# A decoder layer in fp32 on one core: two column parts of the output projection as one pass of Strassen's seven products

## The chip, the core and the metric

The kernel runs on one core of a Trainium2 chip. A core has a matrix engine (PE), a vector engine (DVE), an activation engine (ACT), a general engine (POOL, GpSimd) and an engine that issues most transfers (SP). Each of them works through its own list of instructions in order, and semaphores tie the lists together. All operands sit in SBUF, 128 partitions wide; PE accumulates into PSUM banks of 512 fp32 numbers per partition, which the other engines read. The metric is the device time of one execution in microseconds; lower is better.

## The reference

One layer of a hybrid decoder on 512 tokens of width 2048, all in fp32:

```python
h = rmsnorm(x, ln_mix)
sb_q, sb_k, sb_v, sw_q, sw_k, sw_v = split(h @ w_in)
sb_o = stick_breaking_attention(sb_q, sb_k, sb_v)       # 16 heads of 64
sw_o = sliding_window_sink_attention(sw_q, sw_k, sw_v, sinks, slopes)  # 16 heads, 4 kv heads
mixed = concat(rmsnorm(sb_o, sb_out_norm), rmsnorm(sw_o, swa_out_norm))
x = x + mixed @ w_out                                   # (512 x 2048) @ (2048 x 2048)
gate, up = split(rmsnorm(x, ln_ffn) @ w_gate_up)        # each 512 x 5632
x = x + (silu(gate) * up) @ w_down
return rmsnorm(x, ln_final)
```

The change is in `mixed @ w_out`, in the half that takes `rmsnorm(sw_o)`: 512 x 1024 times 1024 x 2048.

## The kernel before, in words

A matrix product in full precision is made of three matmuls. An operand is split into a rounded part hi (made by ACT as a copy) and a rest lo = operand - hi (made by DVE), and PE adds hi by hi, hi by lo and lo by hi. For weights the two parts are called whi and wlo (`split`, L221 and L222), for the mixed heads mhi and mlo, for the normed input of the feed-forward part hca, hcs, hco and hct.

Plain projections run as a queue of slabs. A slab is 256 rows by 512 columns of a weight, one transfer of 512 KB on SP's queue; its raw tile has three buffers, its whi and wlo two. With 4 token blocks, 2 row blocks and 3 matmuls a slab of the output projection has 24 matmuls of 512 columns in eight steps; four slabs make a column part (`add_outA`, `add_outB`), 96 matmuls. A split is issued one slab ahead. At the end of a part DVE evicts its four PSUM banks with x = rstd * bank + x. Between the steps, `defer(n, fn)` runs a function n steps later.

The gate, up, down and value projections don't run in this way, but as passes of Strassen's seven products with Winograd's sums: left and right operands are cut into 2 x 2 blocks, sums and differences of blocks take the place of one product in eight. In such a pass POOL makes differences of raw weights, ACT copies them to PSUM in rounded form (hp) and again to SBUF (whi), DVE makes wlo from hp. The work is laid out in slots, one for each half of a product, and functions are put at a slot with `at_slot`. The forms are the left operands: of the blocks 11, 12, 21, 22 the products 1, 2, 4 use blocks, the products 7, 5, 6, 3 use s3 = 11 - 21, s1 = 21 + 22, s2 = s1 - 11 and 12 - s2, in place.

The output projection's first half (rows of `w_out` for head group A, four column parts) is filler for the sliding-window attention: 16 blocks (4 groups by 4 token blocks), each with scores, exponentials, transposes (`swa_tr`: PE transposes s into the banks z, ACT copies them as phi, DVE makes plo), and the product with v. `pull(cost)` steps the queue of slabs until that much PE time has passed. After the last block of a group the tile oB holds the group's two head blocks; `sumsq_add` squares them on ACT (oc) and adds them on POOL to sqB, and `mix_split` makes mhi by an ACT copy with the gain as scale (L273) and mlo by a DVE operation (L274).

Then come the four column parts of the second half, `add_outB`, plain. The norm's factor rstdB is computed from sqB (8 small matmuls, L735, and a short chain on DVE and ACT) in the first of them. When a part of x is complete, `h2_split` transposes it (16 PE transposes, L1209, four DVE operations that apply gain and factor, L1214) to the tile xh. From two such tiles `form` makes the seven left operands of the feed-forward part: for s = 0 from parts 0 and 1 inside the third part, for s = 1 from parts 2 and 3 later. Sums are on DVE (L1240 and L1243) except that of product 3 (POOL, L1246), hi parts on ACT (L1253), lo parts on DVE (L1256).

The order within an engine is the compiler's schedule for instructions that are not pinned, and program order for the pinned ones (`pV`, `pA`, `pG`, `pT`, all transfers on SP). In the passes most are pinned.

## Time and profile before

| | us |
|---|---|
| runs | 1989.48, 1989.37, 1988.89 (median 1989.37) |
| profiled execution | 1988.84 |
| its span in the trace | 1987.0 |
| end of the first half's last part, and last window block | 576 to 599.8 |
| second half, parts 0 and 1 | 599.8 to 647 |
| second half, part 2, with the forms for s = 0 | 647 to 671.7 |
| second half, part 3 | from 671.7 |

The page gives per engine its busy time, its share of the span and its count of instructions; then a digit for each fortieth of the span; then the chain of work that ended last, by engine. Rows of groups read: line, engine, operation, output <- inputs, shape, xcount, then busy time and mean ns of one, then idle time ahead of them and what ended it. Timeline rows read: start in us, duration, then the same. Instructions that directly follow each other and are alike stand in one row (x4), with the duration of the whole. Matmul durations overlap: matmuls of 512 columns start every 0.227 us and are shown as 0.39 each.

### The profile page before, as it was taken

The page shows a single profiled execution, that of the slowest core. Times are in us where ns is not written, and L with a number is a line of the kernel's source. Part 1 is how long each engine was busy: PE and PEld are TensorE (multiplying, and loading weights), DVE is VectorE, ACT ScalarE, POOL GpSimd, SP SyncE. Part 2 cuts the span into 40 slices and gives each one's busy share as a digit, 9 for nine tenths or more (in the row PEclk, how much of TensorE's full clock was granted, in tenths as well). Part 3 has the DMA queues.
Part 4 walks back from the last instruction along what each step waited for, and adds up shares of the span by engine and source line. Part 5 has one row for each costly group of instructions (what it writes and reads, how often), then busy time and mean ns, then how long its engine had stood idle before and what let it go on. Part 6 is the DMA issues. An engine that isn't in the chain of part 4 may idle for free.

```text
span 1987.0 us, 28973 instructions
## 1 busy us (share of the span) xinstructions
PE 1974.1 (99%) x10204; PEld 1687.7 (85%) x10204; DVE 1480.3 (75%) x2053; ACT 1498.5 (75%) x2015; POOL 999.8 (50%) x441
## 2 busy tenths in 40 slices
PE   9999999999999999999999999999999999999998
PEld 8888888898888888888888888888888888888886
DVE  6676888889964787777777777777777867767767
ACT  6775878868753587777777777777777788888887
POOL 2840000000010266657576666657575778878883
PEclk9999999999999999999999999999999999999999
DMA  6415454422342554444545354444534734433523
GB/s 203 148 54 142 97 144 113 121 75 85 96 138 96 172 136 113 127 125 114 137 103 144 101 139 110 129 121 118 135 104 129 279 127 148 149 127 120 177 75 117
DMA packets 290977, 252.81 MB, mean 127 GB/s; under 512 B 12560, under 2 KB 234832, under 8 KB 288400
## 3 DMA queue, kind: packets, MB, share of 16 engines
q1 hardware_dynamic: 289072, 244.11, 42.2%
q0 software_dynamic: 1376, 5.52, 0.9%
q8 instruction: 81, 1.33, 0.3%
q10 hardware_dynamic: 384, 1.34, 0.2%
q14 instruction: 64, 0.52, 0.1%
HBM read 218.40 MB, written 19.92 MB: 120 GB/s over the span
## 4 chain that ended last, share of the span: by engine, by line
PE 97%; ACT 2%; DVE 1%; issue 0%; DVEq 0%; POOL 0%; ACTq 0%; POOLq 0%
PE o L118 36%; PE m L118 30%; PE m L418 3%; PE m L419 3%; PE m L420 3%; PE m L384 2%; PE m L382 2%; PE m L383 2%; PE z L118 1%; PE o L384 1%; PE o L382 1%; PE o L383 1%; PE z L933 1%; PE o L961 1%; PE z L1132 1%; PE z L886 1%
## 5 line engine op out<-in xcount | busy, mean ns | idle before, releaser
L118 DVE TENSOR_TENSOR wlo<-t,hp 128x1024 fp32r<-128x1024 f32 x247 | 301.2, 1219 | 184.6 <-PE o L118 114.2
L118 POOL TENSOR_TENSOR t<-raw,t 128x1024 f32<-128x1024 f32 x111 | 282.2, 2543 | 281.5 <-ACT hp L118 269.6
L118 ACT ACTIVATE whi<-t 128x1024 fp32r<-128x1024 f32 x247 | 262.1, 1061 | 126.4 <-PE o L118 76.4
L118 PE MATMUL o<-hca,whi 128*128 128x512 f32 x880 | 307.5, 391 | 0.0
L118 POOL TENSOR_TENSOR t<-raw,raw 128x1024 f32<-128x1024 f32 x114 | 295.0, 2590 | 21.9 <-issue 11.3
L118 DVE TENSOR_TENSOR wlo<-raw,hp 128x1024 fp32r<-128x1024 f32 x187 | 228.3, 1221 | 93.2 <-issue 52.2
L118 ACT ACTIVATE whi<-raw 128x1024 fp32r<-128x1024 f32 (+1 forms) x189 | 200.0, 1058 | 105.0 <-PE m L118 75.0
L118 ACT ACTIVATE hp<-t 128x1024 fp32r<-128x1024 f32 x247 | 249.2, 1009 | 2.9 <-POOL t L118 2.9
L118 PE MATMUL o<-hca,wlo 128*128 128x256 f32 x880 | 244.0, 280 | 0.0
L118 ACT ACTIVATE hp<-raw 128x1024 fp32r<-128x1024 f32 x191 | 192.9, 1010 | 3.8 <-DVE wlo L118 1.4
L118 PEld LDWEIGHTS o<-hca,whi 128*128 128x128 f32 x880 | 164.2, 187 | 35.8
L118 PE MATMUL m<-hca,whi 128*128 128x512 f32 x528 | 186.3, 392 | 1.1 <-DVE hca L118 1.1
L118 PEld LDWEIGHTS o<-hca,wlo 128*128 128x128 f32 x880 | 165.6, 189 | 0.4
L221 ACT ACTIVATE whi<-raw 128x1024 fp32r<-128x1024 f32 x87 | 91.9, 1057 | 86.1 <-PE o L384 38.6
L222 DVE TENSOR_TENSOR wlo<-raw,whi 128x1024 fp32r<-128x1024 f32 x87 | 109.4, 1258 | 54.7 <-ACT whi L221 52.6
L730 POOL TENSOR_TENSOR sqA<-sqA,oc 128x512 f32<-128x512 f32 x7 | 10.1, 1439 | 273.9 <-ACT oc L729 273.9
L118 PE MATMUL m<-whi,dca 128*128 128x512 f32 x592 | 146.9, 389 | 0.0
L118 PE MATMUL o<-whi,dca 128*128 128x512 f32 x592 | 146.8, 389 | 0.0
L118 PE MATMUL m<-hca,wlo 128*128 128x256 f32 x528 | 146.3, 280 | 0.0
L118 PEld LDWEIGHTS o<-whi,dca 128*128 128x128 f32 x592 | 111.1, 188 | 23.0
L118 PEld LDWEIGHTS m<-whi,dca 128*128 128x128 f32 x592 | 111.0, 188 | 23.1
L118 PE MATMUL m<-hcs,whi 128*128 128x512 f32 x352 | 125.9, 392 | 0.0
(364 smaller groups left out, 5187.5 us busy)
## 6 DMA issues: line engine op xcount, KB each, us to landing
raw<-in_w_gate_up_dram SPq DMA_DIRECT2D x348, 256.0 KB, 5.2
raw<-in_w_down_dram SPq DMA_DIRECT2D x68, 512.0 KB, 5.0
raw<-in_w_in_dram SPq DMA_DIRECT2D x35, 512.0 KB, 4.5
raw<-in_w_in_dram SPq DMA_DIRECT2D x66, 256.0 KB, 3.9
raw<-in_w_out_dram SPq DMA_DIRECT2D x32, 512.0 KB, 3.7
aT<-w SPq DMA_DIRECT2D x44, 256.0 KB, 3.4
xd<-aT SPq DMA_DIRECT2D x10, 1024.0 KB, 6.7
rx<-in_w_down_dram SPq DMA_DIRECT2D x20, 512.0 KB, 5.7
```

Of the source, the lines that this page charges most:

```text
L118: return lambda *a, **k: tc.keep_in_program_order(fn(*a, **k))
L221: A.activation(out=hi, in_=raw, func=AF.Copy)
L222: V.tensor_tensor(out=lo, in0=raw, in1=f(hi), op=ALU.subtract)
L382: mm(o, lhsT=lh[:, sl], rhs=hi[:, j, :], start=first, stop=False, skip_group_check=halves)
L383: mm(o, lhsT=lh[:, sl], rhs=lo[:, j, :], start=False, stop=False, skip_group_check=halves)
L384: mm(o, lhsT=ll[:, sl], rhs=hi[:, j, :], start=False, stop=(k == nslab * a - 1), skip_group_check=halves)
L418: mm(o, lhsT=wh, rhs=xh, start=(k == 0), stop=False)
L419: mm(o, lhsT=wh, rhs=xl, start=False, stop=False)
L420: mm(o, lhsT=wl, rhs=xh, start=False, stop=(k == KT - 1))
L886: mm(out, lhsT=kb, rhs=H.q2[:, c0:S], start=False, stop=True, skip_group_check=True)
L933: mm(zb[:, o:o + r.shape[1]], lhsT=lhsT, rhs=r, start=False, stop=last, skip_group_check=True)
L961: mm(H.ob[:, c0:S], lhsT=vb, rhs=r[:, o:o + S - c0], start=(k == 3 and r is B.h), stop=(k == 0 and r is B.l), skip_group_check=True)
```

## The change

The first two column parts of the second half become one pass of seven products (`OutPass`, a `Block` as in the other passes). Its left blocks are halves of the tokens by halves of the 1024 rows, its right blocks are the two column parts by the same halves: 7 products, 2 halves each, 12 matmuls of 512 columns per half. Four of its left operands need sums of oB, so oB must be multiplied by the gain ahead: POOL does that in place after the last block of a group. `split_b` then makes mhi and mlo of two head blocks at a time, where `mix_split` made one. The last three slabs of the first half's last part are held back from the window blocks and run in the pass's six preparatory slots, four steps in each. The parts 2 and 3 stay plain. The transposes of parts 0 and 1, their sums of squares and the forms for s = 0 move into part 2, and of these forms POOL now makes the sums of 5 and 6 and the lo parts of 1, 2, 4 and 3 in addition to the sum of 3.

```diff
+    obs = ExitStack()
+    obp = obs.enter_context(tc.tile_pool(name="obp", bufs=1))
+    oB = [obp.tile([P, 4, 512], F32, name=f"oB{n}") for n in range(2)]
     sqB = swp.tile([P, 512], F32, name="sqB", bufs=1)
-    oB = [swp.tile([P, 4, 512], F32, tag="oB", name="oB", bufs=2) for _ in range(2)]
...
+    def split_b(m):
+        hi, lo = mixB[8 + m] = (act8("mhi"), act8("mlo"))
+        for e in (0, 2):
+            A.activation(out=hi[:, e:e + 2, :], in_=oB[m][:, e:e + 2, :], func=AF.Copy)
+            V.tensor_tensor(out=lo[:, e:e + 2, :], in0=oB[m][:, e:e + 2, :], in1=f(hi)[:, e:e + 2, :], op=ALU.subtract)
+        for j in range(4):
+            mixB[4 * m + j] = (hi[:, j, :], lo[:, j, :])
...
-                sumsq_add(sqB, oB[g // 2][:, (g % 2) * 2 + j, :], g == 0 and j == 0, tmp(name="oc"))
+                o = oB[g // 2][:, (g % 2) * 2 + j, :]
+                sumsq_add(sqB, o, g == 0 and j == 0, tmp(name="oc"))
+                G.tensor_scalar(out=o, in0=o, scalar1=gcol[:, 40 + 2 * g + j:41 + 2 * g + j], scalar2=None, op0=ALU.mult)
...
-    pull(2600.0)
+    pull(2600.0, a_end - 3)
...
+        if j == 13:
+            split_b(0)
+        pull(SWFILL / 4, a_end - 3)
+    split_b(1)
+    drain(a_end - 3)
     kqs.close()
-    rstdB = sumsq_rstd(sqB, "rstdB")
...
+    class OutPass(Block):
...
+        def sum(self, p, i):
+            self.difference(p, i, self.raw["12", i] if p == "5" else self.t["6", i] if p == "4" else
+                            self.tile("t", [P, 2, 512], bufs=3))
...
+        def add(self, p, eng):
+            b = self.block
+            if p == "7":
+                self.s3 = self.tile("t", [P, 2, 512], bufs=3).rearrange("p u (a b) -> p (u a) b", a=2)
+                eng.tensor_tensor(out=self.s3, in0=b("11"), in1=b("21"), op=ALU.subtract)
+            elif p == "5":
+                eng.tensor_tensor(out=b("21"), in0=b("21"), in1=b("22"), op=ALU.add)
+            elif p == "6":
+                eng.tensor_tensor(out=b("11"), in0=b("21"), in1=b("11"), op=ALU.subtract)
+            else:
+                eng.tensor_tensor(out=b("12"), in0=b("12"), in1=b("11"), op=ALU.subtract)
+
+        def form(self, p, eng=None):
+            src = self.s3 if p == "7" else self.block({"5": "21", "6": "11", "3": "12"}[p])
+            if eng is None:
+                self.f[p] = self.tile("vf", [P, 4, 512], F32R, 2)
+                pA.activation(out=self.f[p][:, :, 0:256], in_=src, func=AF.Copy)
+            else:
+                hl = self.f[p]
+                eng.tensor_tensor(out=hl[:, :, 256:512], in0=src, in1=f(hl)[:, :, 0:256], op=ALU.subtract)
+
+        def take(self, p):
+            bk = self.bank[{"6": "1", "4": "7", "3": "5"}.get(p, p)]
+            if p == "6":
+                self.u.append(self.tile("vu", [P, 2, 512]))
+            for t in range(2):
+                if p == "6":
+                    pV.tensor_copy(out=self.u[0][:, t, :], in_=bk[t])
+                else:
+                    c, h = {"1": (0, 0), "7": (1, 2), "4": (0, 2), "5": (1, 2), "2": (0, 0), "3": (1, 0)}[p]
+                    out = x2[c][:, h + t, :]
+                    pV.scalar_tensor_tensor(out=out, in0=bk[t], scalar=rstd_b[0][:, h + t:h + t + 1], in1=out,
+                                            op0=ALU.mult, op1=ALU.add)
+
...
+    open_phase("op", 1, reuse_waits="tile")
+    bp = OutPass()
...
+    for k, q, i in ((-6, "22", 0), (-6, "12", 0), (-5, "11", 0), (-4, "11", 1), (-3, "12", 1), (-2, "22", 1),
+                    (0, "21", 0), (1, "21", 1)):
+        at_slot(k, "load", bp.load, q, i)
+    for k, fn, *args in ((-5, bp.add, "7", pG), (-4, bp.sum, "7", 0), (-3, bp.add, "5", pV), (-3, bp.sum, "5", 0),
+                         (-2, bp.form, "7", pV), (-2, bp.add, "6", pV), (-1, bp.sum, "6", 0), (-1, bp.add, "3", pV),
+                         (0, bp.sum, "7", 1), (1, bp.sum, "5", 1), (2, bp.form, "6", pG), (3, bp.sum, "6", 1),
+                         (4, bp.sum, "4", 0), (5, bp.sum, "4", 1), (6, bp.form, "5", pG), (8, bp.form, "3", pG)):
+        at_slot(k, "sum", fn, *args)
+    for k, p in ((-4, "7"), (0, "6"), (4, "5"), (7, "3")):
+        at_slot(k, "late", bp.form, p)
+    for k, p in enumerate(PD):
+        at_slot(2 * k + 2, "take", bp.take, p)
+    for k, c, h in ((8, 1, 0), (9, 0, 2), (11, 1, 2)):
+        for t in range(2):
+            at_slot(k + t, "late", bp.add_u, c, h, t)
...
+    def b_slot(n):
+        run(n, "load")
+        run(n, "sum")
+        bof(n + 1, "to_hi")
+        bof(n + 1, "to_lo")
+        bof(n + 2, "to_hp")
+
+    for n in range(-6, 0):
+        if n == -4:
+            rstd_b.append(sumsq_rstd(sqB, "rstdB", pz()))
+        if n == -2:
+            open_z("psb")
+        b_slot(n)
+        for _ in range(4):
+            step()
+        run(n, "late")
...
             elif p == "5":
                 src = a21
-                eV.tensor_tensor(out=src, in0=a21, in1=a22, op=ALU.add)
+                (eV if s else G).tensor_tensor(out=src, in0=a21, in1=a22, op=ALU.add)
             elif p == "6":
                 src = a11
-                eV.tensor_tensor(out=src, in0=a21, in1=a11, op=ALU.subtract)
+                (eV if s else G).tensor_tensor(out=src, in0=a21, in1=a11, op=ALU.subtract)
             elif p == "3":
                 src = a12
                 (pG if s else G).tensor_tensor(out=src, in0=a12, in1=a11, op=ALU.subtract)
...
-            eV.tensor_tensor(out=hl[:, :, 256:512], in0=src, in1=f(hl)[:, :, 0:256], op=ALU.subtract)
+            (G if s == 0 and p in "1243" else eV).tensor_tensor(out=hl[:, :, 256:512], in0=src, in1=f(hl)[:, :, 0:256],
+                                                                op=ALU.subtract)
...
-                if c == 1:
-                    defer(12, lambda: [form(p, 0) for p in PR])
...
-                lambda k: mixB[k], lambda: four(1), done, mix_prep(mixB, oB, 40))
-    add_outB(0)
-    outB0 = len(queue)
-    for c in range(1, 4):
+                lambda k: mixB[k], lambda: four(1), done)
+    for c in (2, 3):
         add_outB(c)
-    drain(outB0)
+    for n in range(14):
+        b_slot(n)
+        if n == 9:
+            load(a_end)
+        if n == 12:
+            load(a_end + 1)
+        if n == 13:
+            split(a_end)
+        bof(n, "product")
+        run(n, "take")
+        run(n, "late")
+    run(14, "take")
+    dma(out=x2s[0], in_=x2[0])
     phase[0].close()
+    obs.close()
     right = ExitStack()
     side = right.enter_context(tc.tile_pool(name="side", bufs=1, side="right", reuse_waits="tile"))
+    open_z("pszb")
+    defer(2, lambda: h2_split(0))
+    defer(3, lambda: [norm_sums(0, t) for t in range(NT)])
+    defer(5, lambda: dma(out=x2s[1], in_=x2[1]))
+    defer(8, lambda: h2_split(1))
+    defer(9, lambda: [norm_sums(1, t) for t in range(NT)])
+    defer(14, lambda: [form(p, 0) for p in PR])
```

Three places show how the order of the engines' lists changes. In all rows the names behind <- are inputs, and "waits" lists the engines or queues whose semaphores the instruction waits for.

The first is DVE at the end of the first half's last part. x_5944 or x_5976 is that part's x, m and o are its banks, sst to rstdB is the norm's factor. Before, from the wlo of that part's last slab:

```order
L222 TENSOR_TENSOR wlo<-raw,whi 128x1024 [waits DMAHW0_49,Activation_49]
L222 TENSOR_TENSOR wlo<-raw,whi 128x1024 [waits DMAHW1_49,Activation_49]
L1061 SCALAR_TENSOR_TENSOR x_5944<-m,rstdA,x_5944 128x512 [waits DMASW5_49,PE_49]
L1061 SCALAR_TENSOR_TENSOR x_5944<-m,rstdA,x_5944 128x512 [waits PE_49]
L1061 SCALAR_TENSOR_TENSOR x_5944<-o,rstdA,x_5944 128x512 [waits PE_49] x2
L738 COPY sst<-o 128x4 [waits PE_49]
L278 TENSOR_SCALAR rv<-sst 128x4 [waits DVE_49]
L222 TENSOR_TENSOR wlo<-raw,whi 128x1024 [waits DMAHW2_49,Activation_49]
L284 TENSOR_TENSOR rt<-rr 128x4 [waits Activation_49]
```

After, from the middle of the norm's chain; the second row ahead of oB's is the wlo of the last slab, oB_4120 and oB_4121 are the tiles of groups 0, 1 and 2, 3, the last row is the wlo of the pass's first product:

```order
L284 TENSOR_TENSOR rt<-rr 128x4 [waits Activation_49]
L285 TENSOR_TENSOR rt<-rt,rv 128x4 [waits DVE_49]
L286 TENSOR_SCALAR rt<-rt 128x4 [waits DVE_49]
L288 TENSOR_TENSOR rstdB<-rr,rt 128x4 [waits DVE_49]
L222 TENSOR_TENSOR wlo<-raw,whi 128x1024 [waits DMAHW2_49,Activation_49]
L118 TENSOR_TENSOR oB_4120<-oB_4120,oB_4121 128x4x256 [waits Pool_49]
L118 TENSOR_TENSOR vf<-t,vf 128x4x256 [waits Activation_49]
L118 TENSOR_TENSOR oB_4120<-oB_4120 128x4x256 [waits DVE_49]
L1073 SCALAR_TENSOR_TENSOR x_5976<-m,rstdA,x_5976 128x512 [waits DMASW5_49,PE_49]
L1073 SCALAR_TENSOR_TENSOR x_5976<-m,rstdA,x_5976 128x512 [waits PE_49]
L118 TENSOR_TENSOR oB_4121<-oB_4121,oB_4120 128x4x256 [waits DVE_49]
L118 TENSOR_TENSOR wlo<-rx,hp 128x1024 [waits DMAHW3_49,Activation_49]
```

The norm's chain has moved ahead of the last slab's wlo, and three sums of oB and a lo form (vf) now stand around the part's evictions.

The second place is ACT after the last block of group 2 in the window attention, before:

```order
L1122 ACTIVATE s<-s,den 128x256 [waits Activation_49]
L273 ACTIVATE mhi<-oB,gcol 128x512
L1135 ACTIVATE phi<-z 128x512 [waits PE_49]
L273 ACTIVATE mhi<-oB,gcol 128x512
L1135 ACTIVATE phi<-z 128x512 [waits PE_49]
L221 ACTIVATE whi<-raw 128x1024 [waits DMAHW3_49,PE_49]
```

and after:

```order
L1135 ACTIVATE s<-s,den 128x256 [waits Activation_49]
L1148 ACTIVATE phi<-z 128x512 [waits PE_49]
L1059 ACTIVATE mhi<-oB_4121 128x1024 [waits Pool_49]
L1148 ACTIVATE phi<-z 128x512 [waits PE_49]
L221 ACTIVATE whi<-raw 128x1024 [waits DMAHW3_49,PE_49]
```

The two scaled copies that waited for nothing new have become one of double width, which waits for POOL, with a phi behind it.

The third place is ACT in the third column part of the second half, where the rows of L221 are whi of its slabs and of the next part's first. Before:

```order
L1253 ACTIVATE hcs<-xh 128x4x256 [waits DVE_49]
L221 ACTIVATE whi<-raw 128x1024 [waits DMAHW5_49,PE_49]
L1253 ACTIVATE hca<-xh 128x4x256 [waits DVE_49]
L1253 ACTIVATE hca<-xh 128x4x256
L221 ACTIVATE whi<-raw 128x1024 [waits DMAHW6_49,PE_49,Activation_49]
L1253 ACTIVATE hca<-xh 128x4x256 [waits DVE_49]
L1253 ACTIVATE hca<-xh 128x4x256 [waits Pool_49]
L221 ACTIVATE whi<-raw 128x1024 [waits DMAHW7_49,PE_49,Activation_49]
```

After, with the forms' hi parts in other places among the whi (the last two rows are the part's fourth slab and the first slab of the next part):

```order
L1390 ACTIVATE hcs<-xh 128x4x256 [waits DVE_49,Pool_49]
L1390 ACTIVATE hcs<-s_6563 128x4x256 [waits DVE_49]
L221 ACTIVATE whi<-raw 128x1024 [waits DMAHW3_49,PE_49]
L1390 ACTIVATE hcs<-xh 128x4x256 [waits DVE_49]
L1390 ACTIVATE hca<-xh 128x4x256 [waits Pool_49]
L1390 ACTIVATE hca<-xh 128x4x256
L1390 ACTIVATE hca<-xh 128x4x256 [waits Pool_49] x2
L221 ACTIVATE whi<-raw 128x1024 [waits DMAHW6_49,PE_49]
L221 ACTIVATE whi<-raw 128x1024 [waits DMAHW7_49,DVE_49,PE_49]
```

POOL's list there, which before held one sum (L1246), is now:

```order
L1393 TENSOR_TENSOR hcs<-xh,hcs 128x4x256 [waits Activation_49]
L1377 TENSOR_TENSOR xh<-xh 128x4x256 [waits DVE_49]
L1380 TENSOR_TENSOR xh<-xh 128x4x256 [waits Pool_49]
L1393 TENSOR_TENSOR hcs<-xh,hcs 128x4x256 [waits Activation_49]
L1383 TENSOR_TENSOR xh<-xh 128x4x256 [waits Pool_49]
L1393 TENSOR_TENSOR hca<-xh,hca 128x4x256 [waits Activation_49] x2
```

The rows of L1377, L1380 and L1383 are the sums of 5, 6 and 3, those of L1393 lo parts. All seven hi parts now stand ahead of the whi of the fourth slab, the last two of them behind a wait for POOL.

More of the change, by code (lines that the diff above doesn't have):

```diff
@@ L730, in sumsq_add, with sumsq_rstd @@
             G.tensor_tensor(out=acc, in0=acc, in1=t, op=ALU.add)
-    def sumsq_rstd(acc, name):
-        pb = po()
+    def sumsq_rstd(acc, name, pb=None):
+        pb = po() if pb is None else pb
         for t in range(NT):
@@ L1067, in tile_hymba @@
         add_outA(c)
+    a_end = len(queue)
     def swa_scores(g, blk):
@@ L1176, in tile_hymba, with __init__, tile, acc @@
         at(swa_av, j - 2)
-        pull(SWFILL / 4)
+        pull(SWFILL / 4, a_end - 3)
         at(swa_norm, j)
         at(swa_scores, j + 1)
-        pull(SWFILL / 4)
-    drain()
-    kqs.close()
-    rstdB = sumsq_rstd(sqB, "rstdB")
+        if j == 13:
+            split_b(0)
+        pull(SWFILL / 4, a_end - 3)
+    split_b(1)
+    drain(a_end - 3)
+    kqs.close()
+    class OutPass(Block):
+        def __init__(self):
+            Block.__init__(self, 0, 0, 0, [], "6")
+            self.f = {}
+        def tile(self, tag, shape, dt=F32, bufs=1):
+            return phase[1].tile(shape, dt, tag=tag, name=tag, bufs=bufs)
+        def acc(self, c):
+            return x2[c]
+        def load(self, q, i):
+            r, c = int(q[0]) - 1, int(q[1]) - 1
+            if q in ("11", "21"):
+                if i == 0:
+                    self.raw[q] = o8.tile([P, 4, 512], F32, tag="o8", name="rx")
+                raw = self.raw[q][:, 2 * i:2 * i + 2, :]
+            elif q == "22":
+                raw = wp.tile([P, 2, 512], F32, tag="raw", name="raw", bufs=RAWB)
+            else:
+                raw = self.tile("raw2", [P, 2, 512], bufs=2)
+            r0 = SBW + (r * 4 + 2 * i) * P
+            dma(out=raw, in_=wout[r0:r0 + 2 * P, c * 512:(c + 1) * 512].rearrange("(a p) c -> p a c", p=P))
+            self.raw[q, i] = raw
+        def sum(self, p, i):
+            self.difference(p, i, self.raw["12", i] if p == "5" else self.t["6", i] if p == "4" else
+                            self.tile("t", [P, 2, 512], bufs=3))
+        def left(self, p, k, half, c):
+            if p in "124":
+                q = {"1": (0, 0), "2": (0, 1), "4": (1, 1)}[p]
+                c += q[0] * 256
+                return mixB[8 + q[1]][half][:, k, c:c + P]
+            c += half * 256
+            return self.f[p][:, k, c:c + P]
+        def block(self, q):
+            return oB[int(q[1]) - 1][:, :, 0:256] if q[0] == "1" else oB[int(q[1]) - 1][:, :, 256:512]
+        def add(self, p, eng):
[24 more added lines that the diff above has]
+                    pV.tensor_copy(out=self.u[0][:, t, :], in_=bk[t])
+                else:
+                    c, h = {"1": (0, 0), "7": (1, 2), "4": (0, 2), "5": (1, 2), "2": (0, 0), "3": (1, 0)}[p]
+                    out = x2[c][:, h + t, :]
+                    pV.scalar_tensor_tensor(out=out, in0=bk[t], scalar=rstd_b[0][:, h + t:h + t + 1], in1=out,
+                                            op0=ALU.mult, op1=ALU.add)
+        def add_u(self, c, h, t):
+            out = x2[c][:, h + t, :]
+            pV.scalar_tensor_tensor(out=out, in0=self.u[0][:, t, :], scalar=rstd_b[0][:, h + t:h + t + 1], in1=out,
+                                    op0=ALU.mult, op1=ALU.add)
@@ new lines, in tile_hymba, with bof @@
+    rstd_b = []
+    open_phase("op", 1, reuse_waits="tile")
+    bp = OutPass()
+    def bof(n, what):
+        if 0 <= n < 14:
+            getattr(bp, what)((PD[n // 2], n % 2))
+    for k, q, i in ((-6, "22", 0), (-6, "12", 0), (-5, "11", 0), (-4, "11", 1), (-3, "12", 1), (-2, "22", 1),
[6 more added lines that the diff above has]
+        at_slot(k, "sum", fn, *args)
```

11 lines of the change are left out of this document (7 added, 4 removed).

## The prediction

> **What bounds the kernel now.** I read the page's busy shares and chain first, then PE's own waits, then four stretches around the change: the end of the first half's fourth column part, the second half's first two parts, its third, and the start of the fourth.
>
> ```profile
> span 1987.0 us, 28973 instructions
> PE 1974.1 (99%) x10204; PEld 1687.7 (85%) x10204; DVE 1480.3 (75%) x2053; ACT 1498.5 (75%) x2015; POOL 999.8 (50%) x441
> PE 97%; ACT 2%; DVE 1%; issue 0%; DVEq 0%; POOL 0%; ACTq 0%; POOLq 0%
> ...
> PE o L118 <- POOL ones L127: 1.2, 1, 1.2
> PE m L118 <- DVE hca L118: 1.1, 1, 1.1
> ...
> 576.00:599.80 23.80, 23.80 (x111) 19.82 (x110) 11.83 (x14) 8.07 (x10) 4.19 (x4) 1.00 0.56 177
> 599.80:647.00 47.20, 47.20 (x218) 39.26 (x217) 22.95 (x29) 16.25 (x29) 0.00 (x0) 1.00 0.28 92
> 647.00:671.70 24.70, 24.70 (x119) 20.66 (x118) 20.94 (x20) 11.79 (x17) 2.40 (x1) 1.00 0.44 149
> ```
>
> PE sets the end. Its two longest waits in 1987 us are 1.2 and 1.1 us, and in these stretches it is busy all the time at clock 1.00 (columns of the last rows: us, then PE, PE loads, DVE, ACT, POOL, clock, DMA share, GB/s). So a removed matmul is worth its full pitch, and anything that makes PE wait costs its full length. POOL has nothing to do in the second stretch; the change fills it.
>
> **A, the matmuls removed.** Two column parts were 2 x 96 matmuls of 512 columns; the pass has 7 x 2 x 12 = 168.
>
> ```profile
> 624.92 1.75 PE z L1209 x16
> 648.49 1.75 PE z L1209 x16
> ```
>
> Between these two groups of transposes lies one part: (648.49 - 624.92 - 1.75)/96 = 0.227 us each. 24 fewer: **-5.45 us**. Everything else is what PE may now wait for.
>
> **How DVE and POOL stand to each other.** This decides most of the sum.
>
> ```profile
> 657.41 1.22 DVE L1243 TENSOR_TENSOR xh<-xh 128x1024 f32<-128x1024 f32 x1
> 658.94 3.33 DVE L222 TENSOR_TENSOR wlo<-raw,whi 128x1024 fp32r<-128x1024 f32 x1 [0.31 <-ACT whi L221]
> 658.78 2.40 POOL L1246 TENSOR_TENSOR xh<-xh 128x1024 f32<-128x1024 f32 x1 [72.97 <-DVE xh L1243]
> ...
> 708.16 2.38 DVE L118 TENSOR_TENSOR hca<-xh,hca 128x1024 fp32r<-128x1024 f32 x1
> 707.07 2.40 POOL L118 TENSOR_TENSOR xh<-xh 128x1024 f32<-128x1024 f32 x1 [2.25 <-DVE xh L118]
> 709.42 6.75 POOL L118 TENSOR_TENSOR t<-raw,raw 128x1024 f32<-128x1024 f32 x2
> ...
> L118 DVE TENSOR_TENSOR wlo<-t,hp 128x1024 fp32r<-128x1024 f32 x247 | 301.2, 1219 | 184.6 <-PE o L118 114.2 <-PE m L118 70.4
> L118 DVE TENSOR_TENSOR dca<-xd,dca 128x1024 fp32r<-128x1024 f32 x10 | 23.7, 2372 | 0.0
> ```
>
> A DVE operation of 1024 elements takes 1.22. When it reads both inputs from SBUF and starts under a POOL operation of 2.40, it ends 1.09 (658.94 + 3.33 - 658.78 - 2.40) or 1.07 after POOL's end: it has done all its work after POOL. POOL's two differences at 709.42 take 6.75, not 4.8: POOL waits its turn as well. So the two alternate, at about 3.5 us a pair. With one input in PSUM (hp) the mean over 247 is the plain 1.219, with two in SBUF beside a busy POOL 2.372. The Trainium skill, "SBUF — State Buffer", section "Who interferes with whom", says the same: a DVE instruction with two SBUF inputs contends with a GpSimd instruction that reads SBUF. By it the three tiny operations of the rstd chain that have two inputs would each wait for a POOL operation too; in C below the last slab's wlo would then come 6.2 late and that of product 1 only 1.8 more, 8.0 instead of 7.5.
>
> **B, the gain multiplies in the window blocks.** After the last block of a group ACT multiplied oB by gain itself; now its 1024-wide mhi waits for POOL to add a square, multiply, add, multiply, and phi, oc and the exponentials stand behind it in ACT's order.
>
> ```profile
> 551.67 2.65 POOL L730 TENSOR_TENSOR sqB<-sqB,oc 128x512 f32<-128x512 f32 x2 [27.67 <-ACT oc L729]
> 554.25 0.59 ACT L1135 ACTIVATE phi<-z 128x512 fp32r<-128x512 f32 x1
> 559.18 0.91 ACT L1122 ACTIVATE s<-s,den 128x256 f32<-128x256 f32 x2 [0.71 <-DVE den L1117]
> 560.67 1.03 PE L1132 MATMUL z<-ident,s 128*128 128x128 f32 x8
> 515.45 2.67 POOL L730 TENSOR_TENSOR sqB<-sqB,oc 128x512 f32<-128x512 f32 x2 [27.45 <-ACT oc L729]
> 520.46 0.59 ACT L1135 ACTIVATE phi<-z 128x512 fp32r<-128x512 f32 x1
> 521.08 0.69 DVE L1136 TENSOR_TENSOR plo<-z,phi 128x512 fp32r<-128x512 f32 x1
> 521.81 0.28 PE L1081 MATMUL z<-kst,qst 128*128 128x256 f32 x1
> L118 POOL TENSOR_TENSOR x2r<-x2r,gf 128x512 f32<-128x512 f32 x8 | 10.4, 1299 | 18.6 <-ACT junk L118 18.4
> L832 POOL TENSOR_SCALAR_AFFINE_SELECT dist<-dist 128x256 f32<-128x256 f32 x1 | 0.4, 410 | 0.1
> L137 POOL TENSOR_SCALAR_AFFINE_SELECT scr<-ones 128x128 f32<-128x128 f32 x1 | 0.3, 304 | 0.0
> 653.64 1.99 ACT L1253 ACTIVATE hca<-xh 128x1024 fp32r<-128x1024 f32 x2
> ```
>
> No row has POOL's multiply by a column. Above it lies the two-input 1.30; below it the selects, 0.304 at 128 elements and 0.410 at 256, which extend to 0.62 at 512. I take 1.0, between them, since the form has one input but runs on the engine whose every 512-wide row is 1.30 or more. The Trainium skill, "GPSIMD Engine Reference", section "3.1 Elementwise — side-by-side cycle accounting", gives 769 ns for 512 elements of a one-input loop; an estimate of B from that page is 2.7.
>
> The third group (552 us): POOL ends at 551.67 + 2.65 + 2.0 = 556.32, mhi takes 0.96 (half of 1.99 less the start-up), phi starts at 557.3 and not at 554.25. ACT was packed from there to 558.28, then DVE's den, s at 559.18 to 560.09, transposes at 560.67: 3.0 late less 0.6 of slack is 2.4. The second group (515 us): POOL ends at 520.1, mhi 521.1, two phi, the second 1.1 late; plo ended at 521.77 and the scores that need its bank ran at 521.81, so 1.1. The first group's mhi stands behind a whole block's exponentials on ACT, and the fourth's feeds only the pass. **+3.5** (2.0 to 4.7 by the two ends).
>
> **C, the start of the pass.** POOL now does s3 and the differences from about 588.5 without a pause; DVE has, in order, mlo, the rstd chain, wlo of the last slab, the sums of 5, the lo of 7, the sum of 6, two evictions, the sum of 3, wlo of product 1.
>
> ```profile
> 582.09 2.99 POOL L730 TENSOR_TENSOR sqB<-sqB,oc 128x512 f32<-128x512 f32 x2 [1.48 <-ACT oc L729]
> 593.20 0.39 PE L382 MATMUL m<-whi,mhi 128*128 128x512 f32 x1
> 598.64 0.95 PE L735 MATMUL o<-ones,sqB 128*128 128x2 f32 x8
> ```
>
> From 582.09: two sums, two multiplies, one turn of wlo and a DMA issue end at 588.5. s3 to 590.9, mlo to 592.1, a difference to 594.7, wlo of the last slab to 595.9. PE wants it 0.23 after 593.20 + 0.95 (the norm's matmuls now lie ahead): 1.4 late. Then difference, sum of 5 (599.5), difference, lo of 7 (603.0), sum of 6 (604.1), and only then the first eviction (604.9), for which product 1 has waited since 593.20 + 0.95 + 1.4 + 24 x 0.227 = 601.0: 3.9, and 0.4 for the second bank. The sum of 3 takes one more turn, wlo of product 1 comes at 608.8, and PE, with seven or eight hi by hi matmuls (1.7) behind it since 605.3, has waited 1.8 for it. **+7.5**. Without turns the same list, one operation behind the other at 1.13 each, leaves 0.2 at the slab's wlo and 0.7 at that of product 1: 0.9.
>
> Inside the pass DVE has per half of a product (12 matmuls, 2.72 us) a wlo of 1.22, which reads hp in PSUM and takes no turns, an eviction of 0.75 and now and then one of the six additions, 2.3 us where it has most; POOL has 8 operations of 2.40 in 38 us. The feed-forward units work in the same way under a heavier load without a wait of PE:
>
> ```profile
> 800.00:850.00 50.00, 50.00 (x290) 44.05 (x290) 36.93 (x43) 39.29 (x44) 34.16 (x14) 1.00 0.37 99
> ```
>
> So I cost the inside at nothing; PE covers it, and each us by which DVE fell behind there would be a us of PE. At the end the next part's first bank waits for the last product's eviction, 0.75 behind an addition of 0.67, while PE has the first transposes to do: **+0.2**. The loads of w_out are as many and as large as before, on SP's queue, ahead of need by four slots and more; no term for them (the windows' DMA shares are 0.28 to 0.56).
>
> **D, the third column part.** Before, its DVE made the sums of 5 and 6 and all lo parts, POOL one sum. Now POOL does lo of 1, sums 5, 6, lo of 2, sum 3, lo of 4 and 3 in this order, and ACT has the hi of 3 ahead of whi of the part's fourth slab.
>
> ```profile
> 648.96 2.73 DVE L1214 SCALAR_TENSOR_TENSOR xh<-z,gcol,rbc 128x512 f32<-128x512 f32 x4 [1.43 <-PE z L1209]
> ```
>
> Let T be the start of the second tile's transposes. PE wants that whi at T + 1.75 + 2 x 24 x 0.227 = T + 12.65. The tile itself is done at T + 0.47 + 2.73 = T + 3.2 by this row, 0.9 later because the lo of 7 now precedes it on DVE, and 1.1 more because that lo waits for POOL's lo of 1: T + 5.2. POOL's four steps to the sum of 3 are 4 x 2.40, and three DVE operations (a wlo, lo of 5, lo of 6) take turns among them: 9.6 + 3.3 = 12.9. Then hi and whi, 2 x 0.96 + 0.1: T + 20.1, 7.5 late, and wlo behind it 1.2 more. **+8.7**; without turns T + 4.1 + 9.6 + 2.0, 3.1 late and 1.0: +4.1. The fourth slab was covered before by DVE; nothing else covers it now.
>
> **Sum.** -5.45 + 3.5 + 7.5 + 0.2 + 8.7 = +14.45 on the profiled 1988.84 (span 1987.0 and 1.84 around it): 2003.3. The median of the runs is 0.53 above that execution: **2003.8**.
>
> **Rivals.** (1) *Turns cost little*: the lengthened rows are single cases, and POOL and DVE mostly miss each other. Then -5.45 + 3.5 + 0.9 + 0.2 + 4.1 = +3.2, 1992.6; for it, the gate and value passes of this kind run beside a POOL busy for most of their time with PE never waiting; against it, the ten dca of 2.372. (2) *Faster*: PE waits nowhere, because POOL does the new 4 x 256 blocks and the multiply in about half its rows' time. It decides in the third part: whi must start by T + 11.6 and hi of 3 takes 1.0 before it, so from T + 4.1 POOL's four steps may take 6.5 and not 9.6. Then phi is at 554.7, inside its slack, and A alone is left with the 0.2: 1984.1. Against it stands the 2.40 at 658.78, the same shape. (3) *Slower still*: POOL's multiply takes 2 us or more, since nothing here shows it. Then B is (551.67 + 2.65 + 4.0 + 0.96 - 554.25 - 0.6) + 3.1 = 7.5, and POOL's start in C 2.0 later: +20.5, 2009.8.
>
> **How the numbers follow.** The forecast gets 0.69, its own range 1998 to 2008 from B's ends and D with one turn more or less; (1) 0.13, (2) 0.10, (3) 0.08. The range, 1991 to 2008.5, takes in most of (1). What this kernel's measurement can tell from no change is about 0.2%, 4.0 us: faster means under 1985.4, slower over 1993.3. Faster is (2) with 0.09 of its 0.10, the same is its rest and two thirds of (1), 0.10; slower is what is left, 0.81.
>
> **What would show it.** PE's waits should name DVE's evictions and wlo at the start of the pass, ACT's whi in the third part (7 to 8 us in one piece), and DVE or ACT behind phi after groups two and three. The DVE rows of the pass's sums should read 2.3 to 3.6 and not 1.22. If they read 1.22, the turns were wrong and (1) holds; if PE's waits sum to less than 6, the whole sum is.

## The result and the profile after

The changed kernel takes 2013.8 us (median of four runs, 2012.63 to 2016.01) against 1989.24 us before: a ratio of 1.0125, with a 95% interval of 1.0107 to 1.0142. It is slower, as forecast, but by 24.6 us and not by 14.5, and outside the stated range. Two executions among those behind the numbers below ran far slower than all others of their kernel (2178 us at a granted clock of 0.85, and 4806 us for the kernel before) and are left out of the medians. The page of the changed kernel, its clock row included:

```profile
span 2011.0 us, 29006 instructions
PE 1977.6 (98%) x10180; PEld 1687.2 (84%) x10180; DVE 1504.2 (75%) x2065; ACT 1520.3 (76%) x2035; POOL 1062.3 (53%) x467
...
PEclk9999999999999899999999999999999999999999
...
PE 93%; ACT 2%; DVE 2%; POOL 1%; DMA 1%; issue 1%; SPq 0%; DVEq 0%; ACTq 0%; POOLq 0%
```

24 matmuls are gone, and yet PE is busy for 3.5 us more. The slice of the clock row that shows 8 is where that comes from. PE's waits (who waits, for whom, us in total, times, longest):

```profile
PE m L382 <- ACT whi L221: 11.0, 2, 6.7
PE z L1145 <- DVE s L1137: 3.3, 1, 3.3
PE z L1094 <- DVE plo L1149: 2.1, 1, 2.1
PE m L118 <- DVE x L1073: 1.4, 1, 1.4
PE m L118 <- DVE wlo L118: 1.3, 1, 1.3
...
PE m L383 <- DVE wlo L222: 0.6, 1, 0.6
```

These 19.7 us are new, at the three places that the prediction named, and they are what it had added up (19.7 without its 0.2 for the end of the pass). The rest stands in the clock column of stretches around two of the waits (us; PE, loads, DVE, ACT, POOL; clock; DMA share; GB/s), and in single matmuls:

```profile
600.00:602.20 2.20, 2.19 (x10) 1.49 (x8) 0.90 (x6) 0.41 (x2) 0.00 (x0) 1.00 1.00 346
602.20:606.50 4.30, 0.00 (x0) 0.00 (x0) 0.00 (x1) 1.09 (x2) 2.34 (x1) 0.86 1.00 342
606.50:609.00 2.50, 2.48 (x6) 2.00 (x7) 2.50 (x2) 2.50 (x3) 2.15 (x1) 0.50 1.06 397
...
670.00:676.70 6.70, 6.70 (x30) 5.26 (x29) 3.27 (x3) 3.10 (x4) 6.62 (x3) 1.00 0.27 81
676.70:683.40 6.70, 0.08 (x1) 0.00 (x0) 2.48 (x1) 1.99 (x3) 6.62 (x3) 0.77 0.00 0
683.40:686.00 2.60, 1.97 (x4) 1.26 (x5) 2.55 (x2) 0.96 (x2) 2.60 (x2) 0.50 0.00 0
686.00:688.50 2.50, 2.50 (x8) 1.92 (x7) 2.50 (x2) 0.00 (x0) 1.00 (x1) 0.50 0.00 0
...
676.39 0.39 PE L384 MATMUL o<-whi,mlo 128*128 128x512 f32 x1
683.47 0.80 PE L382 MATMUL m<-whi,mhi 128*128 128x512 f32 x1 [6.69 <-ACT whi L221]
687.56 0.63 PE L383 MATMUL m<-wlo,mhi 128*128 128x512 f32 x1
687.98 0.63 PE L384 MATMUL m<-whi,mlo 128*128 128x512 f32 x1
690.81 0.40 PE L382 MATMUL o<-whi,mhi 128*128 128x512 f32 x1
```

After three of these waits the granted clock is 0.50 for 4 to 7 us, and matmuls of 512 columns start every 0.427 us (687.56 to 687.98) and not every 0.227. So I measure a place not by its wait but from the last matmul start before it to the first at full pitch after it, less what the matmuls between take at 0.227: from 676.39 to 690.81 there are 16 pitches, 3.63 us, and 14.42 went by, 10.8 lost.

| place | predicted | waits | lost |
|---|---|---|---|
| window block after group 2 | 1.1 | 2.1 | 2.3 |
| window block after group 3 | 2.4 | 3.3 | 5.2 |
| first half's last slab | 1.4 | 4.3 | 7.2 |
| start of the pass | 6.1 | 1.4 and 1.3 | 3.6 |
| third part, fourth slab | 8.7 | 6.7 and 0.6 | 10.8 |
| sum | 19.7 | 19.7 | 29.1 |

Less 5.45 for the removed matmuls that is 23.6; the feed-forward part's first wait for hca moved from 710.60 to 734.99, by 24.4. The 0.8 us between are gaps of 0.3 us and less in other places. The pass itself loses nothing once it runs: its last 152 matmuls take from 621.97 to 656.42, 0.2266 each. Behind that point both kernels take the same time to 0.4 us.

Two more views are needed for the steps. The third part's chain on POOL and what follows it on ACT:

```profile
669.00 3.31 POOL L1377 TENSOR_TENSOR xh<-xh 128x1024 f32<-128x1024 f32 x1 [3.80 <-DVE xh L1351]
672.39 2.41 POOL L1380 TENSOR_TENSOR xh<-xh 128x1024 f32<-128x1024 f32 x1
674.76 3.34 POOL L1393 TENSOR_TENSOR hcs<-xh,hcs 128x1024 fp32r<-128x1024 f32 x1
678.18 3.20 POOL L1383 TENSOR_TENSOR xh<-xh 128x1024 f32<-128x1024 f32 x1
...
681.41 1.06 ACT L1390 ACTIVATE hca<-xh 128x1024 fp32r<-128x1024 f32 x1 [5.51 <-POOL xh L1383]
682.37 1.99 ACT L221 ACTIVATE whi<-raw 128x1024 fp32r<-128x1024 f32 x2
```

It is the chain of the prediction: 12.4 us for four steps (12.9 predicted), then hi of 3, then whi. And the start of the pass:

```profile
595.63 0.95 PE L735 MATMUL z<-ones,sqB 128*128 128x2 f32 x8
596.66 0.88 SPq L100 DMA_DIRECT2D raw<-in_w_out_dram  x2
605.41 1.06 ACT L221 ACTIVATE whi<-raw 128x1024 fp32r<-128x1024 f32 x1 [4.66 <-DMA raw<-in_w_out_dram]
602.83 2.34 POOL L118 TENSOR_TENSOR t<-raw,raw 128x1024 f32<-128x1024 f32 x1 [3.92 <-DMA raw<-in_w_out_dram]
606.85 3.12 POOL L118 TENSOR_TENSOR raw<-raw,rx 128x1024 f32<-128x1024 f32 x1 [1.68 <-DMA rx<-in_w_out_dram]
607.64 3.41 DVE L118 TENSOR_TENSOR oB<-oB,oB 128x1024 f32<-128x1024 f32 x1
610.98 3.40 DVE L118 TENSOR_TENSOR vf<-t,vf 128x1024 fp32r<-128x1024 f32 x1
...
L1168 POOL TENSOR_SCALAR oB<-oB,gcol x8: 1558/1563/2529, 479.7 to 594.1; 128x512 f32<-128x512 f32 x8
```

SP issued nothing between 579.09 and 596.66. The first load that then goes out is the pass's, into memory of the window attention's pool, which sqB still occupied until PE's eight small matmuls had read it (595.63 to 596.58); the last slab's load stood behind it and came with seven others, and with POOL's own transfer of 1 MB of x (issued at 595.63), at 340 to 400 GB/s. DVE and POOL take turns as forecast (3.4 where 1.22 was the plain time). Of the two only DVE reads PSUM banks in this trace; POOL's inputs are in SBUF, so each of its operations can meet a DVE operation with two inputs there. And POOL's multiply by a column takes 1.56 us (minimum, median and maximum ns in the last row).

### The profile page after: what moved, and what is told of

The parts are those of the page before. It is cut to its first block, busy times and chain, and to the rows that moved or that the text cites. A ratio compares the mean times of both kernels' runs of the same rounds, so it can differ in the third digit from the quotient of the medians.

```text
span 2011.0 us, 29006 instructions
## 1 busy us (share of the span) xinstructions
PE 1977.6 (98%) x10180; PEld 1687.2 (84%) x10180; DVE 1504.2 (75%) x2065; ACT 1520.3 (76%) x2035; POOL 1062.3 (53%) x467
## 4 chain that ended last, share of the span: by engine, by line
PE 93%; ACT 2%; DVE 2%; POOL 1%; DMA 1%; issue 1%; SPq 0%; DVEq 0%; ACTq 0%; POOLq 0%
PE o L118 37%; PE m L118 31%; PE m L418 3%; PE m L419 3%; PE m L420 3%; PE z L118 1%; PE z L933 1%; PE m L383 1%; PE m L384 1%; PE m L382 1%; PE o L961 1%; PE o L382 1%; PE o L383 1%; PE o L384 1%; PE z L886 1%
## 5 line engine op out<-in xcount | busy, mean ns | idle before, releaser
L118 DVE TENSOR_TENSOR wlo<-t,hp 128x1024 fp32r<-128x1024 f32 x253 | 308.5, 1219 | 188.0 <-PE o L118 114.4
L118 ACT ACTIVATE whi<-t 128x1024 fp32r<-128x1024 f32 x253 | 268.4, 1061 | 127.0 <-PE o L118 76.8
L118 POOL TENSOR_TENSOR t<-raw,raw 128x1024 f32<-128x1024 f32 x118 | 306.0, 2596 | 28.6 <-issue 11.0
L118 DVE TENSOR_TENSOR wlo<-raw,hp 128x1024 fp32r<-128x1024 f32 x191 | 233.1, 1220 | 94.4 <-issue 52.2
L118 ACT ACTIVATE whi<-raw 128x1024 fp32r<-128x1024 f32 (+1 forms) x193 | 204.2, 1058 | 107.1 <-PE m L118 74.9
L118 ACT ACTIVATE hp<-t 128x1024 fp32r<-128x1024 f32 x253 | 255.2, 1009 | 7.4 <-DVE wlo L118 4.1
L222 DVE TENSOR_TENSOR wlo<-raw,whi 128x1024 fp32r<-128x1024 f32 x79 | 99.4, 1259 | 40.7 <-ACT whi L221 37.9
L221 ACT ACTIVATE whi<-raw 128x1024 fp32r<-128x1024 f32 x79 | 83.3, 1055 | 58.1 <-PE m L419 13.3
```

The lines of the kernel that those rows point to most:

```text
L118: return lambda *a, **k: tc.keep_in_program_order(fn(*a, **k))
L221: A.activation(out=hi, in_=raw, func=AF.Copy)
L222: V.tensor_tensor(out=lo, in0=raw, in1=f(hi), op=ALU.subtract)
```

## The experiments

The theory after the result: the three places are as predicted in kind, each wait costs its length and, if long, a stretch of half clock; in C the first wait is SP's queue. All times are medians against the kernel before on the same chip, 1988.6 to 1989.2 us. The four runs or so of each single edit spread by 1 to 4 us, so a difference of a us or two is not read.

**Forms as before.** Sums of 5 and 6 and all lo parts on DVE again.

```diff
-                (eV if s else G).tensor_tensor(out=src, in0=a21, in1=a22, op=ALU.add)
+                eV.tensor_tensor(out=src, in0=a21, in1=a22, op=ALU.add)
...
-            (G if s == 0 and p in "1243" else eV).tensor_tensor(out=hl[:, :, 256:512], in0=src, in1=f(hl)[:, :, 0:256],
+            eV.tensor_tensor(out=hl[:, :, 256:512], in0=src, in1=f(hl)[:, :, 0:256],
```

> The changed kernel with the forms for s = 0 made as before: sums of 5 and 6 and all lo parts on DVE, the sum of 3 on POOL. Theory (POOL's chain 5, 6, lo of 2, 3 holds ACT's hi of 3, and with it whi of the third part's fourth slab; the clock then falls because PE stood still): the waits of 6.7 and 0.6 us there go, and with them about 3.3 us of matmuls at half clock, so 2013.8 - 10.6 = about 2003, and the granted clock in that part reads 1.00. Rival (DVE, with a lo and sums more, becomes late there, since in the changed kernel the transposes of parts 0 and 1 lie in the same part too): a wait for DVE of 2 to 5 us takes its place, 2006 to 2010.

Measured 2010.5 us: the rival's time. The wait is shorter and has another end:

```profile
672.57 3.49 DVE L1393 TENSOR_TENSOR hca<-xh,hca 128x1024 fp32r<-128x1024 f32 x3
672.82 5.48 POOL L1383 TENSOR_TENSOR xh<-xh 128x1024 f32<-128x1024 f32 x1 [30.41 <-DVE xh L1380]
679.42 1.23 DVE L1393 TENSOR_TENSOR hca<-xh,hca 128x1024 fp32r<-128x1024 f32 x1 [3.37 <-ACT hca L1390]
681.84 0.80 PE L383 MATMUL m<-wlo,mhi 128*128 128x512 f32 x1 [3.95 <-DVE wlo L222]
```

But DVE wasn't too busy: it stood still for 3.37 us. The one sum left on POOL started 0.25 us after a row of three lo on DVE and took 5.48 us; hi of 3, lo of 3 and the slab's wlo came after it.

**Work inside the wait.** 24 matmuls into a bank that nobody reads, between the third and the fourth slab.

```diff
+    def keep_busy(n):
+        pb = pz()
+        hi = queue[a_end + 2]["hi"]
+        for i in range(n):
+            mm(pb, lhsT=mixB[6][0][:, 0:P], rhs=hi[:, i % 2, :], start=True, stop=True)
+
+    defer(24, lambda: keep_busy(24))
```

> The changed kernel with 24 more matmuls of 512 columns in the third part, between its third and fourth slab, into a PSUM bank that nobody reads: 5.45 us of work for PE inside the wait of 6.7 us. Nothing else is changed. Theory (the granted clock falls to one half because PE stood still for longer than some 3 us): PE's wait shrinks to about 1.3 us, the fourth slab begins at the same time as without the added work, but at full clock, and the kernel is about 3 us faster, 2010.5. Rival (the clock falls for another reason, such as load or what POOL and DVE do): the fourth slab still runs at 0.5 and the time stays at 2013.8, or rises where the added matmuls outlast the wait.

2011.8 us, 2.0 less with 24 matmuls more. Stretches of it around the same place:

```profile
676.00:683.00 7.00, 7.00 (x32) 5.79 (x32) 5.55 (x2) 1.79 (x2) 6.92 (x3) 1.00 0.00 1
683.00:686.00 3.00, 1.65 (x9) 1.03 (x7) 0.08 (x1) 2.12 (x3) 3.00 (x2) 1.00 0.00 0
686.00:688.50 2.50, 1.63 (x6) 1.13 (x7) 2.50 (x2) 0.83 (x1) 2.50 (x2) 1.00 0.00 0
```

DVE and POOL do what they did, and the clock stays at 1.00; the fourth slab, from its first start to the next part's, takes 6.7 us and not 9.4. The clock falls because PE stands still. The median lacks 0.7 us to the slab's 2.7; in the profiled execution the pass's wait for the eviction was 2.2 us and not 1.4, with a clock of 0.52 behind it, which is a likely place for it.

**The last slab's load first.**

```diff
+    load(a_end - 1)
     for n in range(-6, 0):
```

> The changed kernel, with the transfer of the last slab of the first half's fourth part issued ahead of the pass's own loads on SP. Theory (the pass's first load into new memory waits for the norm's eight matmuls, which read sqB in the memory of the window attention, and the last slab's load stands behind it on SP's queue): the wait of 4.3 us for whi there goes, and the half clock after it, 2.9 us; 2006 to 2008. Rival (DVE's turns behind POOL were only hidden by that wait): the waits for the evictions and for wlo of product 1 grow from 1.4 and 1.3 to some 4 and 2, and the gain is 3 us or less, 2010 to 2013.

2005.95 us (four runs from 2004.7 to 2009.1), 7.85 less: the theory's time, and the rival's mechanism in part. The wait for whi is gone (0.36 for wlo stays) and that for DVE's eviction is now 3.26 us in one piece:

```profile
609.65 2.22 PE L118 MATMUL m<-whi,mhi 128*128 128x512 f32 x4 [3.26 <-DVE x L1073]
```

In the traced execution, 8.1 us faster than that of the change, 1.7 us of the gain are luck: the wait after group 3 lowered no clock there. So without the late load the turns make waits of about 3.6 us, half of what I had put for C.

**The gain on ACT.**

```diff
-                G.tensor_scalar(out=o, in0=o, scalar1=gcol[:, 40 + 2 * g + j:41 + 2 * g + j], scalar2=None, op0=ALU.mult)
+                A.activation(out=o, in_=o, func=AF.Copy, scale=gcol[:, 40 + 2 * g + j:41 + 2 * g + j])
```

> The changed kernel with oB multiplied by the gain in place on ACT (two scaled copies of 512 for each group) and no longer on POOL. Theory (the 2 x 1.56 us of POOL's multiplies, with ACT's mhi and phi queued behind them, are the waits of 2.1 and 3.3 us after the groups two and three): ACT's copies take 2 x 0.6 and wait for nobody; the waits fall below 1 us in all, and the clock of 0.62 to 0.81 after the 3.3 us goes; 2013.8 - 4.4 - 1.7 = about 2007.5. Rival (ACT itself is packed there and becomes late by its 1.2 us more): a wait of 0.6 to 1.2 us stays after each of the groups, 2009 to 2011.

2002.8 us, 11.0 less and better than the theory. After the groups one wait of 0.3 us is left. The wait of 4.3 for whi is 2.23. SP's first load of the pass still goes out 0.08 us behind the norm's matmuls (588.95 and 589.03), as in the changed kernel (596.58 and 596.66). But POOL, without its last multiplies, issues its 1 MB of x 4.1 us ahead of that load and not 1.0, and the last slab's load lands 6.1 us after its issue and not 8.2. That the two transfers share the bandwidth is a likely reason; no run tests it alone.

**The form of 3 later.**

```diff
-    defer(14, lambda: [form(p, 0) for p in PR])
+    defer(14, lambda: [form(p, 0) for p in PR if p != "3"])
+    defer(22, lambda: form("3", 0))
```

> The changed kernel with only the form of product 3 for s = 0 issued eight steps later, so that on ACT its hi stands behind whi of the third part's fourth slab. POOL's share is kept whole. Theory (that wait is ACT's order behind POOL's chain to the sum of 3, not POOL's load as such): the waits of 6.7 and 0.6 us and the half clock after them go, about 2003. In the run with the forms on DVE it was the same order, hi of 3 and lo of 3 ahead of the slab's whi and wlo, that left 4.0 us. Rival (turns: DVE's wlo of that slab waits for POOL's lo operations): a wait of 2 to 3.5 us for DVE's wlo stays, 2006 to 2009.

2011.3 us, 2.5 less and above even the rival's range. The third part is read in the next run, which has the same edit there.

**Three edits together**: load first, gain on ACT, form of 3 later.

> Three edits together: the last slab's load ahead of the pass's loads, the gain on ACT, the form of product 3 later. Theory (the waits are separate and each costs its length and the clock after it): B's waits gone, C without the load's wait but with evictions of the first half behind DVE's sums, 2.5 to 3.5 us, D gone: 1989.2 - 5.5 + 3.5 = 1987 to 1989 with the clock at 1.00 all through. Rival (the gains overlap, because one wait hid another): a new wait of 3 us or more appears in the pass or behind it, and the time is over 1992.

1994.6 us: the rival's size. Most of what is left lies in the third part, DVE first, then PE:

```profile
658.67 5.76 DVE L1394 TENSOR_TENSOR hca<-xh,hca 128x1024 fp32r<-128x1024 f32 x2 [3.38 <-ACT hca L1391]
664.35 3.35 DVE L222 TENSOR_TENSOR wlo<-raw,whi 128x1024 fp32r<-128x1024 f32 x1
...
667.76 0.80 PE L383 MATMUL m<-wlo,mhi 128*128 128x512 f32 x1 [5.13 <-DVE wlo L222]
```

With ACT's whi in time, the slab's wlo needs 3.35 us for itself and stands behind two lo that need 5.76 for two, each waiting for a POOL operation. ACT's order was only the first of two things that POOL's chain held up.

**Sums in the pass later**, all three behind the evictions, on top of the three edits.

```diff
-    ... (-3, bp.add, "5", pV) ... (-2, bp.add, "6", pV) ... (-1, bp.add, "3", pV) ... (2, bp.form, "6", pG)
+    ... (0, bp.add, "5", pV) ... (1, bp.add, "6", pV) ... (4, bp.add, "3", pV) ... (3, bp.form, "6", pG)
-    for k, p in ((-4, "7"), (0, "6"), (4, "5"), (7, "3")):
+    for k, p in ((-4, "7"), (1, "6"), (4, "5"), (7, "3")):
```

> As the run with the three edits, and in the pass the sums of 5, 6 and 3 on DVE two to five slots later, behind the evictions of the first half's last part, and the hi and lo of 6 one slot later. Theory (those evictions wait only because the sums that take turns with POOL stand ahead of them on DVE): the wait of about 3 us for them falls below 1, and the removed matmuls show: 1984.5 to 1986. Rival (POOL's differences and lo of 6 now come too late for products 7 and 6): a wait for POOL or DVE inside the pass, 1 to 3 us, and 1987 to 1989 as without it.

1994.4 us, no difference: the two waits for evictions and wlo (1.05 and 1.25 us) are gone, and two for ACT's whi (1.22 and 1.24) have come in products 7 and 6. Both expected times were too low, because they left out the third part's wait of 5.1 us, which both runs have.

**The sharing alone**, in the kernel before, with the change's own lines for the sums of 5 and 6 and the lo parts.

> The kernel before, plain column parts and all, with only the forms for s = 0 shared with POOL as in the change (sums of 5 and 6, lo of 1, 2, 4, 3). Theory (POOL's chain lo of 1, 5, 6, lo of 2, 3 of 2.4 us each and its turns with DVE hold hi of 3 on ACT, and whi of the third slab behind it): the second tile is done at 651.7, hi of 3 at about 668 and whi at 669, where PE wants it at about 659: a wait of 9 us and 3 us of half clock, about 2001. Rival (in the kernel before the transposes lie early enough and the sharing alone is free): 1989 to 1991.

1995.4 us, 6.7 more than before (ratio 1.0033, 1.0021 to 1.0046), between theory and rival: the mechanism is there at about half the size.

```profile
666.22 0.79 PE L382 MATMUL m<-whi,mhi 128*128 128x512 f32 x1 [3.10 <-ACT whi L221]
667.58 0.79 PE L383 MATMUL m<-wlo,mhi 128*128 128x512 f32 x1 [0.56 <-DVE wlo L222]
```

I had taken the whi that waits for the third slab's; it is the fourth's, which PE wants 5 us later. 3.7 us of waits cost 6.7 us.

**All forms for s = 0 on DVE**: the edit of the first run, and the sum of 3 too.

```diff
-                (pG if s else G).tensor_tensor(out=src, in0=a12, in1=a11, op=ALU.subtract)
+                (pG if s else V).tensor_tensor(out=src, in0=a12, in1=a11, op=ALU.subtract)
```

> The changed kernel with all sums and all lo parts of the forms for s = 0 on DVE, the sum of 3 too, so that POOL has none of them. Theory (what delays the third part's fourth slab is DVE and POOL holding each other up: with the sum of 3 left on POOL it took 5.48 us beside DVE's lo parts, and hi of 3, lo of 3 and the slab's wlo came after it): without POOL, DVE's eleven operations of 1.13 us, four evictions and two wlo fit in the 15 us before the slab; a wait of 0 to 1 us, no half clock there, 2013.8 - 10.5 = about 2003. Rival (DVE has too much to do there, whoever else is at work): a wait of 2 us or more for wlo, 2006 to 2010.

2004.0 us, 9.8 less than the change and as expected; 0.5 us of wait is left there. More work on DVE makes it faster: without POOL beside it its sums and lo parts take 1.2 us each there.

**Four edits, and two steps more.** The first of these runs has the load first, the gain on ACT, all forms on DVE, and in the pass the sum of 6 at slot 0 and that of 3 at slot 4.

> Four edits: the last slab's load first, the gain on ACT, the forms for s = 0 wholly on DVE, and in the pass the sum of 6 two slots later and that of 3 five slots later (the sum of 5 and the lo of 7 stay). Theory (all waits that the change made are then gone or short, and a short wait costs no clock): waits of the pass and behind it under 2 us in all, 1989.0 - 5.5 + 1.5 = 1985, the clock 1.00 throughout. Rival (moving DVE's sums only moves the wait, as in the run with all three sums later, where ACT's whi of products 7 and 6 came 1.2 us late each): 1987 to 1988.

1987.1 us (ratio 0.9992, 0.9983 to 1.0001). The rival's time: a wait of 1.7 us for ACT's whi has come in the pass. 0.5 us is waited in the third part; the clock is 0.999, as in the kernel before.

```diff
-    defer(8, lambda: h2_split(1))
+    defer(6, lambda: h2_split(1))
```

> As the run before, with the second tile's transposes two steps (1.4 us) earlier in the third part. Theory (the forms are ready that much earlier, and the fourth slab's wlo is the last thing that is late): 0 to 1 us less than the run before. Rival (the transposes then stand in PE's list ahead of a slab whose x isn't complete): PE waits for DVE's evictions of the pass, 1 us more.

1986.3 us (0.9987, 0.9979 to 0.9996): the 0.5 us are gone. The intervals of this run and the one before overlap.

```diff
-                         (0, bp.sum, "7", 1), (1, bp.sum, "5", 1), (2, bp.form, "6", pG), (3, bp.sum, "6", 1),
+                         (0, bp.sum, "7", 1), (1, bp.sum, "5", 1), (2, bp.form, "6", pV), (3, bp.sum, "6", 1),
```

> As the run before (transposes two steps earlier), and the lo of product 6 in the pass on DVE and not on POOL. Theory (the last wait of 1.95 us, for ACT's whi of product 6's second half, is POOL's order: lo of 6 for 2.42 us ahead of the difference that ACT rounds next): the difference is done 2.4 to 3.4 us earlier, the waits of 1.95 and 0.24 us go, 1986.34 - 2.2 = about 1984.2, which is the 5.45 us of the removed matmuls less 0.6. Rival (DVE then falls behind with a wlo, because its lo of 6 takes a turn behind POOL): a wait of 1 to 2 us for DVE in products 7 or 6, 1986.

1984.8 us against 1988.6 (ratio 0.9980, 0.9971 to 0.9989): this version is faster than the changed kernel and, by 3.8 us, than the kernel before. The waits of 1.95 and 0.24 us are gone, and one of 1.2 for ACT's whi has come. Its span and what is left of new waits:

```profile
span 1983.1 us, 29011 instructions
...
PE o L118 <- ACT whi L118: 1.2, 1, 1.2
PE z L1145 <- DVE s L1137: 0.3, 1, 0.3
```

1987.0 - 5.45 + 1.5 = 1983.05, against 1983.1: the pass is worth what its removed matmuls said. That it meets to 0.1 is luck, since the spans of the kernel before alone lie between 1986.1 and 1987.7.

## Why the prediction was wrong

**The step that failed** stands in its first part: "anything that makes PE wait costs its full length". It costs more. The waits added up to the forecast sum, 19.7 us, and cost 29.1. About 1.0 of the difference is bookkeeping (a wait is counted from the end of a pipelined matmul, 0.16 us after the next could have started, six times), and 0.6 lies in the first matmuls behind the two waits at the start of the pass. The rest, near 7.8 us, is matmuls at half clock, and the run with work inside the wait shows that it is the standing still that causes it. That the waits met the forecast sum is luck: B's were 5.4 us for 3.5, C's 7.0 for 7.5, D's 7.3 for 8.7. Every row of the profile before that I had read had a clock of 1.00, and its longest wait was 1.2 us, so none had the price; I read the column and asked nothing about it. The Trainium skill, "TensorE: Matmul & The Clock Gate", section "Part 1: The HAM clock gate (the "warmup" mystery)", has it: the array's clock is halved when a free-running window of 3.4 us shows it idle, and is given back after about as long at work. The traces agree on the half (0.50) and on windows of 3.41 us; a window that was idle for 2.0 us was enough here, see the last section.

**A** was right: the pass runs at 0.2266 us a matmul, and the last run's span fits 5.45 us less.

**B** was mis-sized by its price. Above POOL's multiply I had set the two-input 1.30 as the upper bound; it takes 1.56, which is also twice the 769 ns that the prediction quotes. With 1.56 in the same steps the waits come out at 2.2 and 3.5; they are 2.1 and 3.3. The run with the gain on ACT confirms who waited for whom.

**C** had the right sum for half the wrong reasons. The loads were given "no term", because they lay slots ahead of need; their place in SP's list was right, but I didn't ask what the first load into a new pool waits for, and who stands behind it. That is 4.3 of the 7.0 us. The turns, without it, make 3.6 and not 7.5: the chain had POOL busy without a pause from 588.5, and it had to wait for its loads.

**D** was right in every link (POOL's chain 12.4 for 12.9, wait 7.3 for 8.7), and incomplete: behind ACT's order DVE's order held the same slab, as two runs showed. That the chain is POOL's doing is shown by the runs with all forms on DVE and with the sharing alone.

**The rivals**: none held. The one with turns of no effect fails at the rows of 3.4 us. The slower one, 2009.8, is the nearest in time, but its multiply of 2 us or more isn't there, and the clock, which makes the difference, isn't in it.

## What to carry to other kernels

Where PE sets the end, ask of each wait whether it is long enough to lower the clock: here waits that left PE idle for less than 1.9 us in one window of 3.41 us cost about their own length, and those that left it idle for 2.0 us or more some 1.7 to 3.4 us on top. So three waits of 1 us, well apart, are better than one of 3. Moving work from DVE to POOL didn't add an engine where both read SBUF: two lists of 1.2 and 2.4 us operations became one list of 3.5 us pairs, and taking the work back made the kernel faster. And where a pool takes over the memory of another, its first load can wait for the last reader there, as here, and everything behind it on that queue waits too; what is needed soonest has to be issued ahead of it.
